# Retention scores in a hybrid decoder trunk: one plain float32 product, or three float32r products of high and low parts

## The chip, the cores and the metric

The kernel runs on one core of a Trainium2 chip. The metric is the device time of one execution in microseconds (us), the median of several runs. A core has five engines that work side by side, each with a queue of its own: TensorE (PE; its weight loads are listed as PEld), VectorE (DVE), ScalarE (ACT), GpSimd (POOL) and SyncE (SP). Matrix products land in PSUM, a small memory of eight banks, out of which ACT and DVE read them.

## What is computed

Two layers of a decoder trunk over 512 tokens of width 1024, all in float32. Each layer is a mixer and then a gated MLP with a short convolution. The mixer projects the tokens once (2560 columns) and feeds three groups of heads from it: differential attention, retention, and a causal pooling mixer. The change is in retention, which goes through the sequence in four chunks of 128 tokens with four heads of 32 query and key columns:

```python
def step(state, inp):
    qi, ki, vi = inp
    inner = jnp.einsum('bhqd,bhkd->bhqk', qi, ki) * decay
    o = (jnp.einsum('bhqk,bhkv->bhqv', inner, vi)
         + jnp.einsum('bhqd,bhdv->bhqv', qi * xi, state))
    state = state * chunk_decay + jnp.einsum('bhkd,bhkv->bhdv', ki * zeta, vi)
    return state, o
```

`inner` before the decay is what is called the scores here.

## The kernel before

Most of the work is weight products. A weight tile of 128x1024 is loaded by SP, ACT rounds it to float32r (the high part, L298 or L287), and DVE subtracts that from the original (the low part, L299 or L288). A product in nearly full precision is then three float32r products: high with high, high with low, low with high (`mm3`, L467). The projections of the mixer, its output projection and the two of the MLP run one after the other in this form. `emit_split` keeps six such tiles ahead.

The attention, retention and pooling work is cut into small steps, written as generators, that are put between the weight products. The order of TensorE is written out by hand: `in_order` (L328) ties each product to the one before it. When a step is put in is decided while the program is built: a counter `now` goes up by one for each 512 columns of weight products (`serve`, L362), and each step has a due time in the table `PLACE` (L45). When its due time is reached and the steps that it needs have been issued, it goes into the queues. On ACT, DVE and POOL the tile framework orders the queues by priority, in which these steps are ahead of the weight work by 300, and it places the semaphores by the buffers that instructions share.

Retention of chunk c consists of four such steps, for which `PLACE` has due times r1 (395, 431, 465, 513 for chunks 0 to 3), r2 (425, 439, 479, 523), r3 (427, 445, 497, 531) and r4 (491, 500, 545, 553):
- `ret_1` (L761): two transposes on TensorE put the chunk's queries and keys, turned, side by side into one PSUM bank `b`. POOL clears `qe`, a block matrix of 128x512; ACT copies the four heads of the queries onto its diagonal blocks (L773, 32 partitions each). DVE copies the keys (L774), multiplies the queries by xi (L775) and the untransposed keys by zeta (L770).
- `ret_2` (L778): one product of 128x512 in plain float32 gives the scores of all four heads; DVE multiplies them by the decay (L782), over `qe`.
- `ret_3` (L784): products with the values and the state, the new state, and the norm of the output.
- `ret_4` (L812): the output is transposed, gated, and split into high and low parts (L823, L824).

Steps of others stand between them: attention's `unit_a` to `unit_e` (scores, transposes, values), the gate `gu_done` (L669), and `pool_f`. `k_split` (L635) cuts attention's keys: for each half of the partitions ACT rounds the high part out of a PSUM bank (L637), and DVE subtracts it from the same bank (L638). `finish_token` (L449) squares a bank on ACT (L454) and multiplies it by the gain on DVE (L456).

Buffers: `t4` (L183) gives tiles of 128x1024 out of a pool of two; `ret_1` takes one for qe, the keys, and the two scaled copies. `t2` (L177) gives tiles of 128x512 from eight slots that are taken in turn by role; role p1 has two slots, used by attention's probabilities and by squares and temporaries of `unit_c`, `ret_3` and `ret_4`. PSUM banks of role b are two, in turn.

Of the kernel before, what the change touches and what calls it, by code (L numbers as in the profile page):

```python
# [11 lines left out]
F32 = mybir.dt.float32  # L12
F32R = mybir.dt.float32r
I32 = mybir.dt.int32
AF = mybir.ActivationFunctionType
ALU = mybir.AluOpType
# [4 lines left out]
P = 128  # L21
D = 1024
# [115 lines left out]
def tile_trunk(ctx: ExitStack, tc: tile.TileContext, x, xt, win, wout, wup, wdown, gpost, par, lam, const, out):  # L138
    nc = tc.nc
    te, ve, se, ge, sy = nc.tensor, nc.vector, nc.scalar, nc.gpsimd, nc.sync  # L140
# [4 lines left out]
    t4p = ctx.enter_context(tc.tile_pool(name="t4p", bufs=2))  # L145
    t2p = ctx.enter_context(tc.tile_pool(name="t2p", bufs=1))
# [6 lines left out]
    def nm(s):  # L153
        uid[0] += 1
        return f"{s}_{uid[0]}"
# [6 lines left out]
    def bank(role, shape=(P, 512)):  # L162
        k = role
        if role in BANKS:
            k = BANKS[role][took[role] % len(BANKS[role])]
            took[role] += 1
        return pp.tile(list(shape), F32, tag=f"bank{k}", name=nm(f"ps_{role}"), bufs=1)
# [6 lines left out]
    ROLES = {"any": list(range(8)), "p0": [0, 1, 2], "p1": [3, 4], "aT": [5, 6], "on": [7], "g": [2]}  # L174
    turn = {r: 0 for r in ROLES}

    def t2(role="any", w=512):  # L177
        ring = ROLES[role]
        k = ring[turn[role] % len(ring)]
        turn[role] += 1  # L180
        return t2p.tile([P, w], F32, tag=f"t2_{k}", name=nm("t2"), padded_shape=[P, 512])

    def t4():  # L183
        return t4p.tile([P, D], F32, tag="t4", name=nm("t4"))

    def small(w):
        return sp.tile([P, w], F32, tag="sm", name=nm("sm"), padded_shape=[P, 16])
# [7 lines left out]
    def C(name):  # L195
        lo, hi = _CONST_AT[name]
        return cst[:, lo:hi]
# [130 lines left out]
    def in_order(r):  # L328
        if last_pe[0] is not None:
            tc.add_manual_dep(r.ins, last_pe[0].ins.name, ORDER, reason="order of TensorE")  # L330
        last_pe[0] = r

    def mm(out, lhsT, rhs, **k):
        in_order(te.matmul(out, lhsT=lhsT, rhs=rhs, **k))  # L334

    def tr(out, in_):
        in_order(te.transpose(out, in_, ident))  # L337
# [71 lines left out]
    def head_rsqrt(ss, n, width):  # L409
        v = small(n)  # L410
        ve.tensor_scalar(v, ss, 1.0 / width, EPS, op0=ALU.mult, op1=ALU.add)
        return rsqrt(v, n)


    def norm_token(t):
        ss = small(2)
        h = t4()
        cut = [slice(0, 512), slice(512, D)]
        for i, c in enumerate(cut):
            se.activation(h[:, c], xs[:, t, c], AF.Square, scale=SQ, accum_out=ss[:, i:i + 1])  # L420
        r = row_rsqrt(ss)
        se.activation(h[:, cut[0]], xs[:, t, cut[0]], AF.Copy, scale=r)
        ve.tensor_scalar(h[:, cut[1]], xs[:, t, cut[1]], r, None, op0=ALU.mult)
        return h
# [4 lines left out]
    def row_factors(t):  # L429
        ss = small(2)  # L430
        for i in range(2):
            scr = t2()
            se.activation(scr, xs[:, t, i * 512:(i + 1) * 512], AF.Square, scale=SQ, accum_out=ss[:, i:i + 1])
        row[t] = tiny.tile([P, 1], F32, tag=f"row{t}", name=nm("row"))
        row_rsqrt(ss, row[t])
# [13 lines left out]
    def finish_token(t, ys, gp):  # L449
        ss = small(2)  # L450
        yg = [t2(), t2()]
        for h in range(2):
            scr = t2()
            se.activation(scr, ys[h], AF.Square, scale=SQ, accum_out=ss[:, h:h + 1])  # L454
        for h in range(2):
            ve.tensor_tensor(out=yg[h], in0=ys[h], in1=gp[:, h * 512:(h + 1) * 512], op=ALU.mult)  # L456
        r = row_rsqrt(ss)
        for h in range(2):
            xh = xs[:, t, h * 512:(h + 1) * 512]
            ve.scalar_tensor_tensor(xh, yg[h], r, xh, op0=ALU.mult, op1=ALU.add)  # L460
# [47 lines left out]
    def load_xt(j):  # L508
        xparts[j] = t4()
        sy.dma_start(xparts[j], xt[j])  # L510
# [8 lines left out]

    raws[0] = rp.tile([P, D], F32, tag="raw", name=nm("raw"))  # L520
    xparts[0] = t4()
    state["dma"] = 1
    load_params(0, se)
# [37 lines left out]
    for l in range(DEPTH):  # L561
# [195 lines left out]
        ret = {}  # L757
        st_bd = [None]
        on_of = {}

        def ret_1(c):  # L761
            tok = rtok[c // 2][:, c % 2, :]
            b = bank("b")
            tr(b[:, 0:P], tok[:, 0:P])
            tr(b[:, P:2 * P], tok[:, P:2 * P])
            w = t4()
            qe, kq, kz = w[:, 0:512], w[:, 512:768], w[:, 768:896]
            ge.memset(qe, 0.0)
            zeta = C("zeta").unsqueeze(2).to_broadcast([P, 4, 32])
            ve.tensor_tensor(out=kz.rearrange("p (h d) -> p h d", h=4), in0=tok[:, 128:256].rearrange("p (h d) -> p h d", h=4), in1=zeta, op=ALU.mult)  # L770
            for h in range(4):
                sl = slice(32 * h, 32 * h + 32)
                se.copy(qe[sl, h * P:(h + 1) * P], b[sl, 0:P])  # L773
            ve.tensor_copy(kq[:, 0:P], b[:, P:2 * P])  # L774
            ve.tensor_tensor(out=kq[:, P:2 * P], in0=b[:, 0:P], in1=C("xi"), op=ALU.mult)  # L775
            ret[c] = (qe, kq, kz)

        def ret_2(c):  # L778
            qe, kq, kz = ret[c]
            b = bank("b")  # L780
            mm(b, lhsT=kq[:, 0:P], rhs=qe, start=True, stop=True)
            ve.tensor_tensor(out=qe, in0=b, in1=C("decay"), op=ALU.mult)  # L782

        def ret_3(c):  # L784
            ind, kq, kz = ret.pop(c)
            b = bank("b")
            if c > 0:
                mm(b[:, 0:256], lhsT=kq[:, P:2 * P], rhs=st_bd[0], start=True, stop=False, skip_group_check=True)
            for h in range(4):
                mm(b[:, 64 * h:64 * h + 64], lhsT=ind[:, h * P:(h + 1) * P], rhs=vr[:, c, 64 * h:64 * h + 64],  # L790
                          start=(c == 0), stop=True, skip_group_check=True)
            if c < NT - 1:
                bu = bank("b")
                mm(bu[:, 0:256], lhsT=kz, rhs=vr[:, c, :], start=True, stop=True)
                ns = one.tile([P, 256], F32, tag="state", name=nm("state"), bufs=2)
                bm = C("bm").unsqueeze(2).to_broadcast([P, 4, 64])
                ve.tensor_tensor(out=ns.rearrange("p (h d) -> p h d", h=4), in0=bu[:, 0:256].rearrange("p (h d) -> p h d", h=4), in1=bm, op=ALU.mult)
                if c > 0:
                    ve.scalar_tensor_tensor(ns, st_bd[0], C("cd"), ns, op0=ALU.mult, op1=ALU.add)
                st_bd[0] = ns  # L800
            oc = rtok[c // 2][:, c % 2, :]
            ov = oc.rearrange("p (h d) -> p h d", h=4)
            se.copy(oc, b[:, 0:256])
            sq = t2("p1", 256)
            se.activation(sq, oc, AF.Square)
            ss = small(4)
            ve.tensor_reduce(ss, sq.rearrange("p (h d) -> p h d", h=4), axis=AX.X, op=ALU.add)
            r = head_rsqrt(ss, 4, 64)
            ve.tensor_tensor(out=ov, in0=ov, in1=r.unsqueeze(2).to_broadcast([P, 4, 64]), op=ALU.mult)
            on_of[c] = oc  # L810
# [74 lines left out]
        def retention(c):  # L885
            yield (l, "r1", c), ((l, "r", c), *[(l, "r3", c - 2)] * (c >= 2), *[(l, "r1", c - 1)] * (c >= 1))
            ret_1(c)
            done.add((l, "r1", c))
            yield (l, "r2", c), ()
            ret_2(c)  # L890
            yield (l, "r3", c), [(l, "r3", c - 1)] * (c >= 1)
            ret_3(c)
            done.add((l, "r3", c))
            yield (l, "r4", c), ((l, "g", 0), (l, "g", 1), (l, "a", 4 * c + 3))
            ret_4(c)
            done.add((l, "r4", c))
# [256 lines left out]
```

## Time and profile before

| | us |
|---|---|
| median of three runs | 1147.39 |
| lowest and highest run | 1146.5, 1148.37 |
| the profiled execution | 1147.81 |
| its span, first to last instruction | 1146.0 |

The granted TensorE clock was 0.998 of full speed over the span. How to read the profile's lines: a group gives line, engine, operation, output and inputs by their names, shape and number, then busy time and mean duration of one; a timeline gives start and duration in us, with the idle time before in brackets and what ended it. `t` stands for any tile of t2 or t4, `ps_b` for a bank of role b, `ps_m` for one of the projections. The line of a source view has the shortest, median and longest duration in ns. In a windows view stand, after the stretch and its length, the busy times of PE, PEld, DVE, ACT and POOL with the number of instructions, then the granted clock, the DMA share and GB/s. Matmuls are pipelined: their starts overlap, and differences are taken between ends.

### The profile page before, as it was taken

Reading aid. Unit: us, or ns where it says so; the run is one execution under the profiler, and the core shown is the slowest. Engines: PE = TensorE matmul, PEld = TensorE weight load, DVE = VectorE, ACT = ScalarE, POOL = GpSimd, SP = SyncE. Lnnn points to the kernel's source line nnn. Section 1 sums busy time; section 2 is a strip of 40 time slices with the busy share of each in tenths; the row PEclk is TensorE's granted clock in tenths of the full one; section 3 lists DMA queues with packets and bytes.
Section 4 is the critical chain, followed back from the end, with each engine's and each line's share of the span. In section 5 each row is a group of like instructions: output and inputs, shape, how many; then the busy total and the mean of one; then the engine's idle time right before and its main releaser. Section 6 shows DMA issues by size and latency. Waiting matters only on the chain.

```text
span 1146.0 us, 14829 instructions
## 1 busy us (share of the span) xinstructions
PE 1134.1 (99%) x5474; PEld 944.3 (82%) x5474; DVE 739.4 (65%) x1669; ACT 546.9 (48%) x1049; POOL 12.0 (1%) x20
## 2 busy tenths in 40 slices
PE   9999999999999999999999999999999999999997
PEld 6788878988888888888888888789888888888885
DVE  6988796776566457423777896876856645663224
ACT  6965544564454345313466754454645434442211
POOL 1000000000000000000000000000000000000000
PEclk9999999999999999999999999999999999999999
DMA  8411131332322222224023111313332223222311
GB/s 326 146 58 56 55 118 36 111 129 97 106 92 93 102 101 100 93 97 142 6 101 116 59 63 46 110 45 121 113 108 93 91 97 107 93 88 98 107 38 56
DMA packets 31320, 109.22 MB, mean 95 GB/s; under 512 B 3728, under 2 KB 4240, under 8 KB 31248
## 3 DMA queue, kind: packets, MB, share of 16 engines
q1 hardware_dynamic: 29808, 105.11, 26.7%
q10 hardware_dynamic: 1440, 3.17, 0.8%
q8 instruction: 43, 0.70, 0.2%
q14 instruction: 29, 0.24, 0.1%
HBM read 106.16 MB, written 2.10 MB: 94 GB/s over the span
## 4 chain that ended last, share of the span: by engine, by line
PE 89%; DVE 4%; ACT 4%; DMA 2%; issue 1%; SPq 0%; DVEq 0%; ACTq 0%
PE ps L334 72%; PE ps_m L334 10%; PE ps_b L334 2%; PE ps_o L334 2%; PE ps_b L337 2%; PE ps_s L334 1%; PE ps L337 1%; DMA rt<-in_lam 1%; DMA raw<-in_wout 1%; DVE ks L638 1%; ACT wa L298 1%; DMA raw<-in_win 1%; ACT t L610 0%; ACT t L701 0%; ACT c L628 0%
## 5 line engine op out<-in xcount | busy, mean ns | idle before, releaser
L334 PE MATMUL ps<-ht,wb 128*128 128x512 f32 (+1 forms) x1176 | 305.0, 368 | 0.0
L334 PE MATMUL ps<-ht,wa 128*128 128x512 f32 (+1 forms) x1176 | 304.8, 367 | 0.0
L334 PEld LDWEIGHTS ps<-ht,wa 128*128 128x128 f32 x1176 | 210.3, 188 | 36.5
L334 PEld LDWEIGHTS ps<-ht,wb 128*128 128x128 f32 x1176 | 210.1, 188 | 36.5
L299 DVE SCALAR_TENSOR_TENSOR wa<-raw,par,wa 128x512 fp32r<-128x512 f32 x128 | 95.7, 748 | 144.6 <-ACT wa L298 144.4
L298 ACT ACTIVATE wa<-raw,par 128x512 fp32r<-128x512 f32 x128 | 92.2, 721 | 185.1 <-PE ps L334 173.4
L334 PE MATMUL ps<-wa,c 128*128 128x512 f32 x448 | 126.3, 394 | 0.0
L334 PE MATMUL ps<-wa,ht 128*128 128x512 f32 x352 | 98.2, 392 | 1.3 <-ACT ht L516 1.1
L288 DVE TENSOR_TENSOR wb<-raw,wa 128x1024 fp32r<-128x1024 f32 x38 | 46.6, 1225 | 81.9 <-ACT wa L287 81.9
L299 DVE SCALAR_TENSOR_TENSOR wb<-raw,par,wb 128x512 fp32r<-128x512 f32 x128 | 95.7, 747 | 4.9 <-ACT wb L298 4.8
L334 PEld LDWEIGHTS ps<-wa,c 128*128 128x128 f32 x448 | 83.6, 188 | 18.0 <-issue 1.0
L298 ACT ACTIVATE wb<-raw,par 128x512 fp32r<-128x512 f32 x128 | 91.9, 720 | 4.3 <-PE ps L334 3.1
L334 PE MATMUL ps_m<-wa,ht 128*128 128x512 f32 x288 | 83.6, 398 | 0.0
L334 PE MATMUL ps_m<-wb,ht 128*128 128x512 f32 x288 | 83.3, 397 | 0.0
L287 ACT CAST wa<-raw 128x1024 fp32r<-128x1024 f32 x38 | 40.0, 1052 | 86.7 <-PE ps L334 86.7
L1023 ACT ACTIVATE t<-ps,par 128x512 f32<-128x512 f32 x88 | 67.5, 774 | 24.9 <-PE ps L334 24.9
L334 PEld LDWEIGHTS ps<-wa,ht 128*128 128x128 f32 x352 | 65.7, 188 | 16.1 <-ACT ht L516 1.9
L1024 DVE SCALAR_TENSOR_TENSOR t<-ps,par,t 128x511 f32<-128x511 f32 x88 | 65.2, 745 | 11.8 <-ACT t L1023 11.7
L334 PE MATMUL ps<-wb,c 128*128 128x512 f32 x224 | 71.8, 397 | 0.0
L334 PE MATMUL ps<-wb,ht 128*128 128x512 f32 x224 | 66.3, 389 | 0.0
L1025 DVE SCALAR_TENSOR_TENSOR t<-ps,par,t 128x510 f32<-128x510 f32 x88 | 65.1, 745 | 1.3
L334 PEld LDWEIGHTS ps_m<-wb,ht 128*128 128x128 f32 x288 | 52.5, 188 | 10.1
(185 smaller groups left out, 1415.8 us busy)
## 6 DMA issues: line engine op xcount, KB each, us to landing
raw<-in_wup SPq DMA_DIRECT2D x88, 512.0 KB, 3.5
raw<-in_wdown SPq DMA_DIRECT2D x44, 512.0 KB, 3.4
raw<-in_win SPq DMA_DIRECT2D x39, 512.0 KB, 3.5
raw<-in_wout SPq DMA_DIRECT2D x16, 512.0 KB, 3.5
xs<-in_x SPq DMA_DIRECT2D x4, 512.0 KB, 9.6
gain<-in_gpost ACTq DMA_DIRECT2D x4, 512.0 KB, 4.5
t<-in_xt SPq DMA_DIRECT2D x3, 512.0 KB, 5.8
out<-xs SPq DMA_DIRECT2D x4, 256.0 KB, 2.0
```

Of the source, the lines that this page charges most:

```text
L287: se.copy(h, r)
L288: ve.tensor_tensor(out=lo, in0=r, in1=h.bitcast(F32), op=ALU.subtract)
L298: se.activation(a, x, AF.Copy, scale=sc)
L299: ve.scalar_tensor_tensor(b, x, sc, a.bitcast(F32), op0=ALU.mult, op1=ALU.subtract)
L334: in_order(te.matmul(out, lhsT=lhsT, rhs=rhs, **k))
L337: in_order(te.transpose(out, in_, ident))
L638: ve.tensor_tensor(out=ks[o, :, m, sl], in0=bv[r], in1=ks[r, :, m, sl].bitcast(F32), op=ALU.subtract)
L1023: se.activation(acc, ps, AF.Identity, bias=conv[:, f, 3:4], scale=conv[:, f, 2:3])
L1024: ve.scalar_tensor_tensor(acc[:, 1:S], ps[:, 0:S - 1], conv[:, f, 1:2], acc[:, 1:S], op0=ALU.mult, op1=ALU.add)
L1025: ve.scalar_tensor_tensor(acc[:, 2:S], ps[:, 0:S - 2], conv[:, f, 0:1], acc[:, 2:S], op0=ALU.mult, op1=ALU.add)
```

## The change

The scores are made as the weight products are: queries and keys are cut into a high part in float32r and the remainder, and three float32r products are added up in the bank. `ret_1` takes a second t4 tile, in float32r, of which the left half `qe` holds the queries' high parts and the right half `ql2` their low parts, both cleared by POOL; and a p1 tile `kk` with the keys' high part `kh` and low part `kl`. The decayed scores go to `ind`, in the first tile, and no longer over `qe`. In each head ACT rounds the high part out of bank b and DVE subtracts it from the same place of the bank; then the same for the keys. The keys' copy moves from DVE to ACT. `ret_3` differs only in names, and the due times are as before.

```diff
-    def t2(role="any", w=512):
+    def t2(role="any", w=512, dtype=F32):
         ...
-        return t2p.tile([P, w], F32, tag=f"t2_{k}", name=nm("t2"), padded_shape=[P, 512])
+        return t2p.tile([P, w], dtype, tag=f"t2_{k}", name=nm("t2"), padded_shape=[P, 512])
-    def t4():
-        return t4p.tile([P, D], F32, tag="t4", name=nm("t4"))
+    def t4(dtype=F32):
+        return t4p.tile([P, D], dtype, tag="t4", name=nm("t4"))
...
             tr(b[:, 0:P], tok[:, 0:P])
             tr(b[:, P:2 * P], tok[:, P:2 * P])
-            w = t4()
-            qe, kq, kz = w[:, 0:512], w[:, 512:768], w[:, 768:896]
-            ge.memset(qe, 0.0)
+            w, qe, kk = t4(), t4(F32R), t2("p1", 256, F32R)
+            ind, qx, kz = w[:, 0:512], w[:, 512:640], w[:, 640:768]
+            qe, ql2 = qe[:, 0:512], qe[:, 512:D]
+            kh, kl = kk[:, 0:P], kk[:, P:2 * P]
+            for x in (qe, ql2):
+                ge.memset(x.bitcast(F32), 0.0)
...
             for h in range(4):
                 sl = slice(32 * h, 32 * h + 32)
-                se.copy(qe[sl, h * P:(h + 1) * P], b[sl, 0:P])
-            ve.tensor_copy(kq[:, 0:P], b[:, P:2 * P])
-            ve.tensor_tensor(out=kq[:, P:2 * P], in0=b[:, 0:P], in1=C("xi"), op=ALU.mult)
-            ret[c] = (qe, kq, kz)
+                cut = slice(h * P, (h + 1) * P)
+                se.copy(qe[sl, cut], b[sl, 0:P])
+                ve.tensor_tensor(out=ql2[sl, cut], in0=b[sl, 0:P], in1=qe[sl, cut].bitcast(F32), op=ALU.subtract)
+            se.copy(kh, b[:, P:2 * P])
+            ve.tensor_tensor(out=kl, in0=b[:, P:2 * P], in1=kh.bitcast(F32), op=ALU.subtract)
+            ve.tensor_tensor(out=qx, in0=b[:, 0:P], in1=C("xi"), op=ALU.mult)
+            ret[c] = (qe, ql2, kh, kl, ind, qx, kz)

         def ret_2(c):
-            qe, kq, kz = ret[c]
+            qe, ql2, kh, kl, ind, qx, kz = ret.pop(c)
             b = bank("b")
-            mm(b, lhsT=kq[:, 0:P], rhs=qe, start=True, stop=True)
-            ve.tensor_tensor(out=qe, in0=b, in1=C("decay"), op=ALU.mult)
+            for n, (x, y) in enumerate(((kh, qe), (kh, ql2), (kl, qe))):
+                mm(b, lhsT=x, rhs=y, start=(n == 0), stop=(n == 2))
+            ve.tensor_tensor(out=ind, in0=b, in1=C("decay"), op=ALU.mult)
+            ret[c] = (ind, qx, kz)
```

More of the change, by code (lines that the diff above doesn't have):

```diff
@@ L772, in ret_1 @@
                 sl = slice(32 * h, 32 * h + 32)
-                se.copy(qe[sl, h * P:(h + 1) * P], b[sl, 0:P])
-            ve.tensor_copy(kq[:, 0:P], b[:, P:2 * P])
-            ve.tensor_tensor(out=kq[:, P:2 * P], in0=b[:, 0:P], in1=C("xi"), op=ALU.mult)
-            ret[c] = (qe, kq, kz)
+                cut = slice(h * P, (h + 1) * P)
[5 more added lines that the diff above has]
+            ret[c] = (qe, ql2, kh, kl, ind, qx, kz)
         def ret_2(c):
-            qe, kq, kz = ret[c]
+            qe, ql2, kh, kl, ind, qx, kz = ret.pop(c)
             b = bank("b")
-            mm(b, lhsT=kq[:, 0:P], rhs=qe, start=True, stop=True)
-            ve.tensor_tensor(out=qe, in0=b, in1=C("decay"), op=ALU.mult)
+            for n, (x, y) in enumerate(((kh, qe), (kh, ql2), (kl, qe))):
+                mm(b, lhsT=x, rhs=y, start=(n == 0), stop=(n == 2))
+            ve.tensor_tensor(out=ind, in0=b, in1=C("decay"), op=ALU.mult)
+            ret[c] = (ind, qx, kz)
         def ret_3(c):
-            ind, kq, kz = ret.pop(c)
+            ind, qx, kz = ret.pop(c)
             b = bank("b")
             if c > 0:
-                mm(b[:, 0:256], lhsT=kq[:, P:2 * P], rhs=st_bd[0], start=True, stop=False, skip_group_check=True)
+                mm(b[:, 0:256], lhsT=qx, rhs=st_bd[0], start=True, stop=False, skip_group_check=True)
             for h in range(4):
```

## The prediction

> **What bounds the kernel now.** I read the page's first part, then its chain, then the queues around the eight score products.
>
> ```profile
> span 1146.0 us, 14829 instructions
> ...
> PE 1134.1 (99%) x5474; PEld 944.3 (82%) x5474; DVE 739.4 (65%) x1669; ACT 546.9 (48%) x1049; POOL 12.0 (1%) x20
> ...
> PE 89%; DVE 4%; ACT 4%; DMA 2%; issue 1%; SPq 0%; DVEq 0%; ACTq 0%
> ```
>
> TensorE is busy in 99% of the span and carries 89% of the chain. Its order is written out by hand and stays as it is. So two things count: TensorE time that is removed, and any time for which TensorE must now wait, because nothing later has slack to take a wait back. DVE's 65% is a mean. In the six stretches of 6 us in which chunks 1, 2 and 3 make their scores (three for each layer) the windows view shows DVE in the third figure after the comma:
>
> ```profile
> 140.00:146.00 6.00, 6.00 (x30) 4.63 (x29) 5.78 (x27) 3.33 (x8) 0.53 (x1) 1.00 0.00 0
> 151.00:157.00 6.00, 6.00 (x27) 4.61 (x26) 5.97 (x16) 3.29 (x7) 0.00 (x0) 1.00 0.64 203
> 166.00:172.00 6.00, 6.00 (x27) 4.39 (x26) 5.93 (x22) 1.34 (x5) 0.00 (x0) 1.00 0.31 100
> 706.50:712.50 6.00, 6.00 (x30) 4.63 (x28) 5.69 (x27) 3.41 (x8) 0.53 (x1) 1.00 0.00 1
> 717.50:723.50 6.00, 6.00 (x27) 4.57 (x26) 6.00 (x16) 3.39 (x7) 0.00 (x0) 1.00 0.66 199
> 732.50:738.50 6.00, 6.00 (x26) 4.41 (x25) 5.89 (x21) 1.34 (x5) 0.00 (x0) 1.00 0.28 93
> ```
>
> DVE is full there, 5.69 to 6.00 of 6, and both layers look alike. I work on layer 0 and double. The granted clock is 1.00 throughout, so it plays no part.
>
> **Part 1: the products on TensorE.** The timeline of chunk 0's score (start, duration, then the group):
>
> ```profile
> 134.57 0.93 PE L334 MATMUL ps_m<-ht,wa 128*128 128x512 f32 x3
> 135.34 0.86 PE L334 MATMUL ps_m<-ht,wb 128*128 128x512 f32 x3
> 136.04 1.02 PE L334 MATMUL ps_b<-t 128*128 128x512 f32 x2
> 136.50 0.80 PE L334 MATMUL ps_m<-ht,wa 128*128 128x512 f32 x1
> ```
>
> One plain product is two instructions. Ends are the measure, since starts overlap: the group before ends at 136.20 and the score at 137.06, so it takes 0.86 us. Three float32r products of the same 128x512 size end 0.70 apart (135.50 to 136.20). Saved: 0.16 us for a score, 1.3 us for eight. No other TensorE work changes.
>
> **Part 2: cutting into high and low parts.** Before, ret_1 made four ACT copies, then two DVE operations. Now each ACT copy of a head is followed by a DVE subtraction which reads the same PSUM bank, then come kh on ACT, kl and qx on DVE. What do two engines do that read one bank?
>
> ```profile
> L456 DVE TENSOR_TENSOR t<-ps,gain x32: 677/686/693, 184.7 to 1138.9; 128x512 f32<-128x512 f32 x32
> ...
>   ACT t L454: 43.7, 11
> ...
> 59.79 0.69 DVE L638 TENSOR_TENSOR ks<-ps_b,ks 64x512 fp32r<-64x512 f32 x1
> ...
> 60.51 0.58 ACT L637 CAST ks<-ps_b 64x512 fp32r<-64x512 f32 x1 [0.87 <-DVE ks L638]
> ```
>
> The second line is from the list of what ended the idle time before L456. L456 multiplies a bank by the gain; ACT's L454 squares the same bank into another tile. Neither uses the other's result, yet DVE idled 43.7 us, 11 times, until ACT was done. The other direction: in k_split, ACT's L637 of the upper partitions began at 60.51, 0.03 us after DVE's L638 of the lower ones ended (59.79 + 0.69 = 60.48). So reads of one bank by ACT and DVE take turns. Then the new chain can't overlap: copy 0, subtraction 0, copy 1, and so on to copy 3, subtraction 3, kh. The prices of its links:
>
> ```profile
> L773 ACT COPY t<-ps_b x32: 236/257/261, 126.7 to 734.6; 32x128 f32<-32x128 f32 x32
> ...
> L774 DVE COPY t<-ps_b x8: 279/285/292, 128.1 to 735.1; 128x128 f32<-128x128 f32 x8
> ```
>
> A copy is 0.257 us. The 32x128 subtraction isn't in this trace; the nearest is L774, also 128 columns out of PSUM, 0.285. Below it is nothing that small on DVE with PSUM input; if it took only the copy's 0.257, six links would give back 0.1 us a chunk. With 0.03 for each hand-over a round is 0.257 + 0.03 + 0.285 + 0.03 = 0.60 us. From the start T of subtraction 0 to the end of kh: 0.285 + 0.03 + three rounds (1.81) + 0.257 = 2.38 us.
>
> Now the three tight chunks. First chunk 1, in the timeline:
>
> ```profile
> 140.09 0.53 POOL L768 MEMSET t<- 128x512 f32 x1 [75.50 <-ACT rtok L803]
> ...
> 140.50 0.38 PE L337 MATMUL ps_b<-cst,rtok 128*128 128x128 f32 x2
> ...
> 140.98 1.06 ACT L773 COPY t<-ps_b 32x128 f32<-32x128 f32 x4 [0.43 <-PE ps_b L337]
> ...
> 141.71 0.15 DVE L397 TENSOR_TENSOR sm<-sm,sm 128x4 f32<-128x4 f32 x1
> ...
> 142.07 0.29 DVE L774 COPY t<-ps_b 128x128 f32<-128x128 f32 x1 [0.21 <-ACT t L773]
> ...
> 142.80 1.02 PE L334 MATMUL ps_b<-t 128*128 128x512 f32 x2
> ```
>
> The transposes L337 end at 140.88 and the score starts at 142.80, in line with the products before it: 1.9 us for the whole cut. Then chunks 2 and 3:
>
> ```profile
> 152.66 1.04 ACT L773 COPY t<-ps_b 32x128 f32<-32x128 f32 x4
> ...
> 152.82 1.28 DVE L299 SCALAR_TENSOR_TENSOR wb<-raw,ws,wa 128x1024 fp32r<-128x1024 f32 x1
> ...
> 154.09 0.29 DVE L774 COPY t<-ps_b 128x128 f32<-128x128 f32 x1
> 154.29 0.15 DVE L397 TENSOR_TENSOR sm<-sm,sm 128x4 f32<-128x4 f32 x1
> ...
> 155.04 0.59 PE L334 MATMUL ps_b<-t 128*128 128x512 f32 x1
> ...
> 167.20 1.06 ACT L773 COPY t<-ps_b 32x128 f32<-32x128 f32 x4
> ...
> 168.10 0.42 DVE L824 TENSOR_TENSOR c<-t,c 128x256 fp32r<-128x256 f32 x1
> ...
> 168.51 0.28 DVE L774 COPY t<-ps_b 128x128 f32<-128x128 f32 x1
> ...
> 168.94 1.10 PE L334 MATMUL ps_b<-t 128*128 128x512 f32 x2
> ```
>
> Chunk 3's score already waits a little: it lasts 1.10 instead of 1.02, so it really begins at 170.04 - 1.02 = 169.02, which is 0.23 after its operand's copy (L774) ended at 168.79. That 0.23 is my price from last operand to score.
>
> T is where DVE's other work lets subtraction 0 in. I choose for it a place that DVE's queue has today after the first copy has ended (its start plus 0.257): in chunk 1 141.71, where L397 stands; in chunk 2 154.09, where L774 stands behind a weight split (L299) of 1.28 us; in chunk 3 168.51, where L774 stands behind the retention output's low part (L824). New start of the score = T + 2.38 + 0.23:
> - chunk 1: 144.32 instead of 142.80, a wait of 1.5 us;
> - chunk 2: 156.70 instead of 155.04, 1.7 us;
> - chunk 3: 171.12 instead of 169.02, 2.1 us;
> - chunk 0: T = 128.1 (first L774), ready at 130.7, score at 136.04: 5 us spare, no wait.
>
> Sum 5.3 us a layer, 10.6 us for two. Minus 1.3 saved: **+9.3 us**. kl is ready 0.03 + 0.285 after kh, and the two products before it cover 0.47, so it adds nothing unless other DVE work slips in before it.
>
> Bounds. If DVE takes each subtraction at once, T is 0.29 behind the copies' start (141.27, 152.95, 167.49) and the waits are 1.1, 0.5 and 1.1: 2.7 a layer, net +4.1. If on top of my sum one other piece of 512 columns gets between two links in each chunk (0.69, as L638 above), it is 2.1 more a layer, net +13.5. Below nothing the whole cannot go by more than Part 1's 1.3, since nothing else is removed from TensorE and the cut only adds work to ACT, DVE and POOL. My value is nearer the middle because T is taken from rows.
>
> **Part 3: the rest.** The second memset on POOL (0.53) is in front of subtraction 0, not of the copies: chunk 1's pair would run 140.09 to 141.15, before 141.71; POOL is 1% busy and nothing else is queued there. If it were late, at most 0.5 us a chunk. ret_1 now takes both t4 buffers, so chunk c+1 needs chunk c's qe and w free; both are released by r3(c) at the latest, which stands ahead of r1(c+1) in the order for every c, and the memset at 140.09 is already one that follows r3(0). Cost nothing, with the same 0.5 as bound. kk in the p1 ring: between r1 and r2 of a chunk at most one other p1 tile is asked for, nothing waits. Behind the waiting instructions stand, on ACT, the gate's tanh (L677) and weight splits (L298); on DVE, the gate's multiplication (L678), the low halves of splits (L299), and then the decay multiplication (L782), for which r3's products wait. All these are later by as much as TensorE is, so I count no second wait. DVE's added work, some 1.1 us a chunk (four subtractions at 0.285), falls into the waits.
>
> The profiled execution took 1147.81 us around its span of 1146.0, 0.42 above the median of the runs, 1147.39. 1147.81 + 9.3 = 1157.1; against the median 1156.7, which is my time.
>
> **Rivals.**
> 1. *Turns are taken by part of a bank.* If the four copies may run on while subtractions read other partitions, only kh, which reads all, waits for subtraction 3. Then the subtractions follow at 0.20, the step from L774 to the next operation in chunk 2 (154.09 to 154.29). Subtraction 3 can begin at 142.07, 154.69 and 169.11, and kh and the score come 0.285 + 0.03 + 0.257 + 0.23 = 0.80 later: chunk 1 at 142.87, chunk 2 at 155.49, chunk 3 at 169.91; waits 0.1, 0.45 and 0.9, 1.4 a layer, net +1.5: 1148.9, no change that shows. It decides if copy 1 starts before subtraction 0 ends. Against it: L637 at 60.51 and L638 touch different halves of the partitions and still took turns; but both write one tile, so that row isn't clean. The Trainium skill (PSUM — Partial Sum Buffer, section on bank collisions) says just this: two engines need to be kept apart only within the same bank and group of 32 partitions, and each head here is such a group. By that rule this rival would hold; the row at 60.51 speaks the other way. 15%.
> 2. *The cut is covered* because the queues are reordered so that the score's operands come first. Only Part 1 is left: 1147.4 - 1.3 = 1146.1. Chunk 1's 1.9 us against 2.6 speaks against it. 7%.
> 3. *Other work gets into the links more often*: weight splits such as the 1.28 us one in chunk 2 fill the idle time between links and run over. Two pieces of 0.69 a chunk are 4.1 a layer: +17.6, 1165.0. It decides from the second piece that gets in. For it: DVE is full. Against: each piece taken early is one less later. 13%.
>
> The forecast itself has 65%.
>
> **The numbers.** About 0.2% (2.3 us) is what a measurement of this kernel can tell from no change. The range goes from 1148.5, just below rival 1, past the bounds +4.1 (1151.5) and +13.5 (1160.9) to 1163.0, midway from the latter to rival 3. Of the chances it leaves out rival 2 (7%), half of rival 3 (6.5%) and a third of rival 1 (5%). Faster by over 0.2%: only as the tail of rival 2, 3%. Within: the rest of rival 2 and most of rival 1, 16%. Slower: 81%.
>
> **What would show it.** Right: in ret_1, ACT copies and DVE subtractions alternate with idle time on ACT ended by DVE; the first score product of chunks 1 to 3 has a wait of 1.5 to 2.1 us ended by ACT (kh); eight times three products at 0.23 each; TensorE's busy time 1.3 us less of work. Wrong: four copies in a row as now with no DVE wait between (rival 1), or scores in line with their neighbours (rival 2).

## The result and the profile after

| | before | after |
|---|---|---|
| median, us | 1147.34 (6 runs) | 1176.85 (6 runs) |
| lowest and highest | 1146.5, 1148.37 | 1175.15, 1178.71 |
| the profiled execution, us | 1147.81 | 1178.71 |
| its span, us | 1146.0 | 1176.9 |
| granted TensorE clock over the span | 0.998 | 0.986 |

The change costs 29.5 us: the ratio is 1.0254, with an interval of 1.0243 to 1.0265. That is on the side that was forecast, but 20.2 us above the time that was forecast and 13.9 above the top of the range.

The page of after, its span, busy times, and the clock in 40 slices (tenths):

```profile
span 1176.9 us, 14897 instructions
...
PE 1143.2 (97%) x5482; PEld 952.7 (81%) x5482; DVE 751.9 (64%) x1701; ACT 549.9 (47%) x1057; POOL 15.7 (1%) x28
...
PEclk9999979999999999999999999899999999999999
```

Two things are new. TensorE was busy 99% of the span and is busy 97%. And its busy time rose by 9.1 us, from 1134.1 to 1143.2, although the change takes work from it. The clock row says why: a 7 in slice 6 (147 to 177 us) and an 8 in slice 26 (736 to 765 us), which are the stretches of retention in the two layers.

Not all of the difference between these two profiled executions is the change's. The first transposes of chunk 0 end at 128.93 us instead of 126.63, so 2.3 us were there before any changed step ran. Early on TensorE waited 1.67 us here and 1.11 before, and from 21.08 to 24.49 us the clock was 0.50, which the profile of before doesn't have. The profiled execution is the slowest of the six, 1.9 us above their median.

The list of TensorE's waits shows where the 2% went. After the line number stands who ended the wait, then the total in us, the number of times, and the longest:

```profile
PEld ps_b L334 <- issue: 23.6, 6, 6.5
...
PE ps_b L334 <- issue: 12.1, 2, 6.1
PE ps_b L334 <- ACT t L780: 9.1, 4, 3.8
```

Six waits are the six tight scores, chunks 1 to 3 of both layers. L780 is the copy of kh. The matmuls stood still for 12.1 + 9.1 = 21.2 us ahead of them, their weight loads for 23.6 (4.4, 6.5 and 0.9 us a layer; some expectations below name these). The list of before has no wait of a score that it puts down to the cut.

The timelines of TensorE at the scores of chunks 1, 2 and 3 in layer 0 (start, duration, group, idle time before):

```profile
148.91 1.62 PE L334 MATMUL ps_b<-t,t 128*128 128x512 f32 x3 [3.85 <-ACT t L780]
```

```profile
169.67 1.62 PE L334 MATMUL ps_b<-t,t 128*128 128x512 f32 x3 [6.02 <-issue]
```

```profile
186.18 0.93 PE L334 MATMUL ps_b<-t,t 128*128 128x512 f32 x3 [0.69 <-ACT t L780]
```

The waits are 3.85, 6.02 and 0.69 us, where 1.5, 1.7 and 2.1 were forecast. And the same three products last 1.62 us in chunks 1 and 2, 0.93 in chunk 3. The windows of after around chunks 1 and 2, the last one from layer 1, give the clock in the figure after POOL's:

```profile
145.10:149.10 4.00, 0.19 (x1) 0.22 (x2) 3.71 (x20) 1.93 (x4) 0.00 (x0) 0.78 0.00 0
149.50:153.50 4.00, 4.00 (x11) 3.14 (x10) 1.98 (x2) 0.00 (x0) 0.98 (x2) 0.50 0.01 4
163.50:170.00 6.50, 0.48 (x2) 0.36 (x2) 5.46 (x16) 4.80 (x9) 0.00 (x0) 0.83 0.45 141
170.00:174.00 4.00, 4.00 (x10) 3.11 (x10) 3.94 (x9) 0.62 (x1) 0.98 (x2) 0.50 0.17 49
...
751.00:755.00 4.00, 4.00 (x11) 3.12 (x10) 3.94 (x7) 0.63 (x1) 0.98 (x2) 0.51 0.24 73
```

While TensorE waits (first and third row) it does next to nothing; in the 4 us behind each wait it is busy throughout, at half clock. This is the other part of the loss, and no step of the prediction had it.

Now the chain of the cut. ACT in chunk 1 of after; L778 is a copy of a head, L779 a subtraction, L780 kh:

```profile
143.11 0.26 ACT L778 CAST t<-ps_b 32x128 fp32r<-32x128 f32 x1 [0.40 <-PE ps_b L337]
143.56 0.63 ACT L677 ACTIVATE sg<-t 128x512 f32<-128x512 f32 x1 [0.19 <-DVE t L676]
144.22 0.26 ACT L778 CAST t<-ps_b 32x128 fp32r<-32x128 f32 x1
145.10 1.15 ACT L298 ACTIVATE wa<-raw,ws 128x1024 fp32r<-128x1024 f32 x1 [0.63 <-PE ps_m L334]
146.28 0.26 ACT L778 CAST t<-ps_b 32x128 fp32r<-32x128 f32 x1
147.59 0.26 ACT L778 CAST t<-ps_b 32x128 fp32r<-32x128 f32 x1 [1.05 <-DVE t L779]
148.50 0.27 ACT L780 CAST t<-ps_b 128x128 fp32r<-128x128 f32 x1 [0.66 <-DVE t L779]
```

and DVE in the same chunk:

```profile
143.91 0.27 DVE L779 TENSOR_TENSOR t<-ps_b,t 32x128 fp32r<-32x128 f32 x1
...
144.25 0.67 DVE L678 SCALAR_TENSOR_TENSOR sg<-sg,t 128x512 f32<-128x512 f32 x1
...
145.11 0.28 DVE L779 TENSOR_TENSOR t<-ps_b,t 32x128 fp32r<-32x128 f32 x1
...
146.47 0.69 DVE L738 TENSOR_TENSOR t<-ps_o,sm 128x512 f32<-128x512 f32 x1
...
147.27 0.29 DVE L779 TENSOR_TENSOR t<-ps_b,t 32x128 fp32r<-32x128 f32 x1
```

Read the two together. Copy 0, subtraction 0, copy 1, subtraction 1: one engine holds the bank, the other waits, as forecast. But into the gap on ACT between copy 0 and copy 1 went the gate's tanh (L677), between copies 1 and 2 a weight split (L298, 1.15 us); into the gaps on DVE went the gate's multiplication (L678), attention's L738 and eighteen operations of some 0.15 us. Each is in front of the next link in its engine's queue, and where it isn't done in time, the link comes late. From copy 0 to the end of kh it is 148.77 - 143.11 = 5.66 us, where the forecast has 3.1 (140.98 to 144.09).

Which pieces cost something is seen by setting each link's start against the end of the link before it; undisturbed it follows 0.03 us later. The tanh cost nothing: copy 1 starts 0.04 us after subtraction 0 ended (143.91 + 0.27 = 144.18). The split cost copy 2 0.9 us. The rest, 2.1 us, is DVE's: its four subtractions come 0.5, 0.6, 0.7 and 0.3 us late. Chunk 2 is worse, and there it is the other engine; ACT:

```profile
161.10 0.24 ACT L778 CAST t<-ps_b 32x128 fp32r<-32x128 f32 x1
163.01 1.15 ACT L298 ACTIVATE space<-raw,ws 128x1024 fp32r<-128x1024 f32 x1 [1.67 <-DMA raw<-in_wout]
164.18 0.26 ACT L778 CAST t<-ps_b 32x128 fp32r<-32x128 f32 x1
165.57 1.15 ACT L298 ACTIVATE space<-raw,ws 128x1024 fp32r<-128x1024 f32 x1 [1.13 <-DMA raw<-in_wout]
166.74 0.26 ACT L778 CAST t<-ps_b 32x128 fp32r<-32x128 f32 x1
...
169.31 0.27 ACT L780 CAST t<-ps_b 128x128 fp32r<-128x128 f32 x1
```

8.48 us instead of 3.8. Between the first and last copy stand four weight splits and a copy of the pooling part on ACT, a split (L299, 1.28), two of pooling's L681 and four of its L842 (0.67 to 0.69 each) on DVE. By the same reckoning ACT's pieces cost 4.2 us and DVE's 1.6. And two of ACT's splits had to wait for the transfer of their own weights, 1.67 and 1.13 us, with the next copy behind them in the queue: the cut waited for weights that it has nothing to do with. Layer 1 shows the same two (1.59 and 1.29 us). In chunk 3 little else is left to get in:

```profile
183.26 0.26 ACT L778 CAST t<-ps_b 32x128 fp32r<-32x128 f32 x1 [2.15 <-PE ps_b L337]
183.93 0.26 ACT L778 CAST t<-ps_b 32x128 fp32r<-32x128 f32 x1 [0.42 <-DVE t L779]
...
185.15 0.26 ACT L778 CAST t<-ps_b 32x128 fp32r<-32x128 f32 x1 [0.35 <-DVE t L779]
185.77 0.27 ACT L780 CAST t<-ps_b 128x128 fp32r<-128x128 f32 x1 [0.36 <-DVE t L779]
```

Here the rounds are 0.61 us, the forecast's 0.60, and the chain lasts 2.78; from the start of subtraction 0 (183.62) to the end of kh it is 2.42.

### The profile page after: what moved, and what is told of

It reads as the page before. It is cut to its first block, busy times and chain, and to the rows that moved or that the text cites. A ratio compares the mean times of both kernels' runs of the same rounds, so it can differ in the third digit from the quotient of the medians.

```text
span 1176.9 us, 14897 instructions
## 1 busy us (share of the span) xinstructions
PE 1143.2 (97%) x5482; PEld 952.7 (81%) x5482; DVE 751.9 (64%) x1701; ACT 549.9 (47%) x1057; POOL 15.7 (1%) x28
## 4 chain that ended last, share of the span: by engine, by line
PE 91%; DVE 4%; ACT 2%; issue 2%; DMA 1%; SPq 0%; DVEq 0%; ACTq 0%
PE ps L334 71%; PE ps_m L334 12%; PE ps_b L334 2%; PE ps_b L337 2%; PE ps_o L334 1%; PE ps_s L334 1%; DMA raw<-in_win 1%; PE ps L337 1%; DVE ks L638 1%; DVE t L779 0%; ACT t L701 0%; DVE sm L699 0%; DVE ps_s L698 0%; ACT wa L298 0%; ACT ks L637 0%
## 5 line engine op out<-in xcount | busy, mean ns | idle before, releaser
L299 DVE SCALAR_TENSOR_TENSOR wa<-raw,par,wa 128x512 fp32r<-128x512 f32 x128 | 95.7, 748 | 146.1 <-ACT wa L298 145.8
L298 ACT ACTIVATE wa<-raw,par 128x512 fp32r<-128x512 f32 x128 | 92.2, 721 | 186.3 <-PE ps L334 173.4
L299 DVE SCALAR_TENSOR_TENSOR wb<-raw,par,wb 128x512 fp32r<-128x512 f32 x128 | 95.7, 748 | 5.0 <-ACT wb L298 4.9
L298 ACT ACTIVATE wb<-raw,par 128x512 fp32r<-128x512 f32 x128 | 91.8, 719 | 4.3 <-PE ps L334 3.2
```

Of the source, the lines that this page charges most:

```text
L298: se.activation(a, x, AF.Copy, scale=sc)
L299: ve.scalar_tensor_tensor(b, x, sc, a.bitcast(F32), op0=ALU.mult, op1=ALU.subtract)
```

## The experiments

Theory A, after the result: ACT and DVE take turns on the one bank, every turn lets other queued work in front of the next link, TensorE waits for the end of the chain, and behind a wait of some 4 us it runs at half clock. Rivals: the added operations cost by their mere number; or the buffers and clears (second t4 tile, `kk`, second memset) do; or the chain is slow because of DVE's load, turns or no turns. Times are medians; the kernel before beside them had 1147.2 to 1147.6.

**The copies first.** The loop is split, so that ACT makes all five copies before DVE's first subtraction; the operations are the same.

```diff
                 se.copy(qe[sl, cut], b[sl, 0:P])
-                ve.tensor_tensor(out=ql2[sl, cut], in0=b[sl, 0:P], in1=qe[sl, cut].bitcast(F32), op=ALU.subtract)
             se.copy(kh, b[:, P:2 * P])
+            for h in range(4):
+                (the same subtraction)
```

> The same instructions as the changed kernel, but ret_1 makes all five ACT copies first and the five DVE subtractions after them. Theory (ACT and DVE take turns on one PSUM bank, and other work gets between the links of that chain): one hand-over is left, the waits at the scores of chunks 1 to 3 fall from 4.4, 6.5 and 0.9 us to at most 0.5 to 1 each, the clock stays at 1.0, time 1147 to 1151 us. Rival (DVE is full, and the five subtractions are too much work for it, in whatever order): the work is the same, so the time stays above 1170.

Measured 1152.49 us (1151.74 to 1152.68), 1.0042 of before, interval 1.0029 to 1.0054: 24.4 us of the 29.5 are gone, and the time is 1.5 above the range that was expected. ACT in chunk 1:

```profile
140.73 1.06 ACT L778 CAST t<-ps_b 32x128 fp32r<-32x128 f32 x4 [0.39 <-PE ps_b L337]
141.81 0.27 ACT L779 CAST t<-ps_b 128x128 fp32r<-128x128 f32 x1
```

The copies run on as before the change, in 1.35 us, and the granted clock is 0.998 again. So the number of operations isn't the cause; their order on the bank is. Most of what is left is in one row of TensorE's waits (here L783 is the subtraction):

```profile
PE ps_b L334 <- DVE t L783: 4.8, 6, 1.3
```

The second product needs the queries' low parts, and the four subtractions now stand one behind the other in DVE's full queue.

**Two banks.** The same two transposes are made a second time into a bank of another role, and DVE reads that one; ACT and DVE share no bank. The order of the statements is that of the change.

```diff
+            b2 = bank("s" if c < 2 else "o")
+            tr(b2[:, 0:P], tok[:, 0:P])
+            tr(b2[:, P:2 * P], tok[:, P:2 * P])
-                ve.tensor_tensor(out=ql2[sl, cut], in0=b[sl, 0:P], ...
+                ve.tensor_tensor(out=ql2[sl, cut], in0=b2[sl, 0:P], ...
```

> The changed kernel with its order of instructions in ret_1 as it is, but queries and keys are transposed a second time into another PSUM bank (of role s for chunks 0 and 1, o for 2 and 3), out of which DVE reads, while ACT reads the first. Adds 16 transposes of 0.11 us. Theory (the shared bank makes the turns): ACT's copies run on without a wait for DVE, no wait of over 1 us at the scores, time 1147.3 - 1.3 + 1.8 plus 0 to 1 us a chunk = 1148 to 1154 us. Rival (each subtraction must follow its copy anyway, or DVE's load): waits stay, above 1170.

Measured 1156.51 us (1155.76 to 1158.24), 1.0081, interval 1.0067 to 1.0095. The copies ran on in 1.37 to 1.39 us although the subtractions stand between them in the program, and the scores waited for 1.6 us in all in four times. The time still misses its range. The largest wait left is of the experiment's own making: the second transposes of chunk 0 came while the borrowed bank was still in use, on the timeline of TensorE:

```profile
128.97 0.44 PE L337 MATMUL ps_s<-cst,rtok 128*128 128x128 f32 x2 [2.20 <-ACT t L701]
```

Twice that is 4.4 us; without it the time would be near 1152 (an estimate: 1156.5 - 4.4).

**Turns and nothing else.** The kernel before, plain product and all, with one thing added: behind each ACT copy of a head DVE copies one column of that head out of the bank into a scratch tile. No cutting, no new product, no new buffer but that scratch tile.

```diff
                 se.copy(qe[sl, h * P:(h + 1) * P], b[sl, 0:P])
+                ve.tensor_copy(small(1)[sl, 0:1], b[sl, 0:1])
```

> The kernel before, plain product and all, with one more DVE instruction behind each of the four ACT copies of the queries: a copy of a single column of the same PSUM bank into a scratch tile. It adds 4 x 8 instructions of well under 0.2 us to DVE and nothing else. Theory (taking turns on the bank is enough): the copies wait for DVE and DVE's other work gets in between, the scores of chunks 1 to 3 wait 1 to 6 us each, time 1155 to 1175 us. Rival (it is the work of the subtractions, the second memset or the float32r products): within 1 us of 1147.4.

Measured 1171.96 us (1170.73 to 1172.28), 1.0208, interval 1.0194 to 1.0222: 24.8 us for 32 operations of 0.15 us, 4.9 us of work on an engine that is not the bound. ACT in chunk 1 (L773 is the copy of a head, L774 the new one-column copy):

```profile
140.72 0.25 ACT L773 COPY t<-ps_b 32x128 f32<-32x128 f32 x1 [0.44 <-PE ps_b L337]
141.17 0.63 ACT L677 ACTIVATE sg<-t 128x512 f32<-128x512 f32 x1 [0.20 <-DVE t L676]
142.02 0.26 ACT L773 COPY t<-ps_b 32x128 f32<-32x128 f32 x1 [0.22 <-DVE sm L774]
142.74 1.15 ACT L298 ACTIVATE wa<-raw,ws 128x1024 fp32r<-128x1024 f32 x1 [0.46 <-PE ps_m L334]
143.91 0.26 ACT L773 COPY t<-ps_b 32x128 f32<-32x128 f32 x1
144.94 0.26 ACT L773 COPY t<-ps_b 32x128 f32<-32x128 f32 x1 [0.78 <-DVE sm L774]
```

It is the picture of after: the same tanh and the same weight split between the same copies. The copies and the one-column reads share no result; only the bank ties them. Scores waited for 16.8 us, and the clock fell behind the waits here too (0.992 over the span). With this the buffers are out as the main cause, as the number of operations was by the copies first.

**No subtractions.** The change without its five subtractions. It leaves the low parts out and adds high times high a second time, so its scores are others than those of the change; it only shows what the rest costs.

```diff
-                ve.tensor_tensor(out=ql2[sl, cut], in0=b[sl, 0:P], ...
-            ve.tensor_tensor(out=kl, in0=b[:, P:2 * P], ...
-            for n, (x, y) in enumerate(((kh, qe), (kh, ql2), (kl, qe))):
+            for n, (x, y) in enumerate(((kh, qe), (kh, ql2), (kh, qe))):
```

> The changed kernel without the five subtractions of each chunk: the low parts are left out (the scores are high by high, high by zeros, and high by high again), all else stays: two t4 tiles, the p1 tile, two memsets on POOL, the keys' copy on ACT, three float32r products. Theory: only the saving on TensorE is left, 1147.3 - 1.3 = 1146 us, give or take 1. Rival (the two t4 tiles, the second memset or the keys' copy on ACT hold up the scores): the time stays well above 1150, with the waits at the scores ended by POOL or ACT.

Measured 1145.33 us (1144.02 to 1146.66, 11 runs), 0.9982, interval 0.9973 to 0.9991: 2.06 us under before. TensorE's list of waits has no row for a score. So second memset, second t4 tile, `kk`, kh on ACT and the three products together cost nothing and save 2.06; all of the loss hangs on the subtractions. It also marks what this form could bring here if the subtractions cost nothing.

**TensorE kept busy.** The change, with plain products of two constants, 5 in chunk 1 and 7 in chunk 2, put in front of the score into a bank that nobody reads then. They fill the wait; the chain is untouched.

```diff
             b = bank("b")
+            if c in (1, 2):
+                fill = bank("s" if c < 2 else "o")
+                for _ in range((5, 7)[c - 1]):
+                    mm(fill, lhsT=ident, rhs=C("decay"), start=True, stop=True)
```

> The changed kernel with 5 (chunk 1) and 7 (chunk 2) plain float32 products of constants into an unused bank, put on TensorE just ahead of the scores, 4.3 and 6.0 us of work in the time in which it would wait. Theory (after a wait of over 4 us TensorE runs at a granted clock of 0.5 for 3.4 to 6.8 us, which costs about 8 us of the added 29.5): the clock stays at 1.0 there and the time falls to 1168 us, give or take 2; the copies and subtractions alternate as before. Rival (the low clock costs nothing, because the queues on ACT and DVE set the pace there): 1176 us or more.

Measured 1168.73 us (1168.66 to 1169.4), 1.0187, interval 1.0173 to 1.0201: 8.1 us less than the change, for more work on TensorE. Its timeline in chunk 1, and a window right behind:

```profile
142.20 4.45 PE L334 MATMUL ps_s<-cst 128*128 128x512 f32 x10
146.21 1.13 PE L334 MATMUL ps_b<-t,t 128*128 128x512 f32 x3
```

```profile
146.00:150.00 4.00, 4.00 (x22) 3.27 (x21) 2.68 (x5) 0.07 (x1) 0.99 (x2) 1.00 0.01 4
```

The cut's chain is as long as it was (5.67 us in chunk 1), but the clock stays at 1.00 behind it, and 22 matmuls fit into 4 us where 11 did. So some 8.1 us of the 29.5 are the clock's.

**Other work held behind the cut.** In the change, all ACT and DVE work issued after a chunk's cut is ordered behind its last operation, so that it can't get between the links.

```diff
-            se.copy(kh, b[:, P:2 * P])
+            last_act = se.copy(kh, b[:, P:2 * P])
-            ve.tensor_tensor(out=qx, ...
+            last_dve = ve.tensor_tensor(out=qx, ...
+            (every later ACT instruction behind last_act, every later DVE one behind last_dve)
```

> The changed kernel with its chain of copies and subtractions as it is, but all ACT and DVE work that the program issues after a chunk's cut is tied behind the cut's last copy (ACT) and last operation (DVE). In chunks 1 and 2 the weight splits, the tanh and the pooling sums can then no longer get between the links. Theory (turns on the bank open the gaps, and other work that fills them is what makes the wait long): the chains of chunks 1 and 2 shrink from 5.7 and 8.5 us to about 3 to 4, the waits at their scores from 4.4 and 6.5 to 1 to 2 us, the clock stays at 1.0, time 1153 to 1160 us. Rival (the turns alone, ten hand-overs a chunk, cost it, whatever stands between): still 1170 to 1177.

Measured 1167.5 us (1166.58 to 1169.25), 1.0173, interval 1.0159 to 1.0187: missed. In chunk 1 the chain shrank to 4.10 us and the wait to 2.28. Chunk 2 is as it was said, with a chain of 3.01 us and no wait over 0.2 at its score. But splits that had been issued earlier were now late and got into chunk 3's chain, which grew to 8.45 us. TensorE at chunk 3's score:

```profile
175.74 1.62 PE L355 MATMUL ps_b<-t,t 128*128 128x512 f32 x3 [6.38 <-ACT t held:10]
```

**A chain with nothing in it.** As the last one, and the links of chunks 1 to 3 are also ordered behind the ACT and DVE work issued before them.

> The changed kernel with its turns on the bank as they are, but in chunks 1 to 3 the cut's links follow each other on ACT and DVE with nothing in between: work issued earlier is tied ahead of the first link, work issued later behind the last. This mends the run before in which only later work was held back and the wait moved to chunk 3. Theory (two parts: turns give 0.61 us a round, 2.8 us from the first copy to kh; what gets in between made 5.4 and 8.5 us of it in chunks 1 and 2): all chains 2.7 to 2.9 us, no low clock, waits of 1 to 3 us a chunk, since the first link now stands behind all earlier work, time 1152 to 1162 us. Rival (the turns alone make the long waits): chains as before, 1167 or more.

Measured 1182.78 us (1181.81 to 1184.84), 1.0307, interval 1.0293 to 1.0321: the slowest of all, and the expectation wrong; by its time the rival would hold. ACT in chunk 1 (all lines are the helper's; the first two rows and the last are copies 0 and 1 and kh):

```profile
140.43 0.26 ACT held:11 CAST t<-ps_b 32x128 fp32r<-32x128 f32 x1 [0.39 <-PE ps_b L365]
144.10 0.26 ACT held:11 CAST t<-ps_b 32x128 fp32r<-32x128 f32 x1 [3.41 <-DVE t held:11]
...
145.94 0.27 ACT held:11 CAST t<-ps_b 128x128 fp32r<-128x128 f32 x1 [0.36 <-DVE t held:11]
```

From the start of subtraction 0 (143.79) to the end of kh (146.21) it is 2.42 us: the forecast's 2.38 for an undisturbed chain holds, so the rival doesn't. But subtraction 0 had to wait 3.1 us behind copy 0 for DVE's backlog. The work that is kept out from between the links is then in front of them. Most of the loss is in chunk 3, where the score waits 9.04 us: copy 0 stands behind three weight splits on ACT, and ACT was idle for 4.65 and 1.33 us before two of them, until their weights had come. So this run shows how long the chain is by itself, but doesn't price the turns: it adds an order that the change hasn't got.

**Later scores.** The copies-first form with r2 at 425, 448, 483, 530 and r3 at 427, 454, 497, 538.

> The changed kernel with all copies first, as in the run that gave 1152.5, and later due times: r2 at 425, 448, 483, 530 and r3 at 427, 454, 497, 538, that is 2.1, 0.9 and 1.6 us later for the scores of chunks 1 to 3, whose first products still waited 1.6, 0.5 and 1.1 us. Theory (what is left over the run without subtractions, 1145.3, are these waits, and TensorE has weight products to do meanwhile): 1145 to 1148 us. Rival (the later steps only push the wait to r3, whose products wait for the decay, or to the retention output that the output projection needs): 1150 us or more.

Measured 1154.81 us (1154.62 to 1156.66), 1.0064, interval 1.0051 to 1.0076: missed. The waits for the subtractions went, and others took their place: 3.4 us at transposes behind L738, 1.8 and 1.6 us at products behind retention's own later steps.

**One copy and one subtraction.** ACT rounds the whole 128x256 once, DVE subtracts once, and the blocks are filled from those two tiles: the queries' high parts by ACT, the low parts by POOL. The bank changes hands once. r2 at 425, 443, 481, 525; r3 at 427, 449, 497, 533.

```diff
+            se.copy(hi, b[:, 0:2 * P])
+            ve.tensor_tensor(out=lo, in0=b[:, 0:2 * P], in1=hi.bitcast(F32), op=ALU.subtract)
-                se.copy(qe[sl, cut], b[sl, 0:P])
+                se.copy(qe[sl, cut], hi[sl, 0:P].bitcast(F32))
-                ve.tensor_tensor(out=ql2[sl, cut], in0=b[sl, 0:P], ...
+                ge.tensor_copy(ql2[sl, cut], lo[sl, 0:P].bitcast(F32))
```

> The changed kernel with one cut for queries and keys together: ACT copies the bank's 128x256 once, rounded, DVE subtracts it once, and the blocks of qe and ql2 are copied out of SBUF, the high parts by ACT and the low parts by POOL. The bank changes hands once, and DVE has two operations a chunk as before the change. r2 and r3 of chunks 1 to 3 are due 0.9, 0.5 and 0.5 us later. Theory: nothing waits for over 0.5 us, 1145 to 1148 us. Rival (POOL's block copies, or ACT's ninth to thirteenth, become the late operand): waits at the scores ended by POOL or ACT, 1149 to 1156 us.

Measured 1152.95 us (1152.35 to 1153.92), 1.0046, interval 1.0032 to 1.006: missed. The turns are gone, but now POOL's copies end the wait, 3.8 us in four times; the four of chunk 3 took

```profile
168.35 3.31 POOL L782 CAST t<-t 32x128 fp32r<-32x128 f32 x4 [9.95 <-DVE sm L398]
```

**The same with ACT for both.** `se.copy` instead of `ge.tensor_copy`.

> As the kernel that cuts queries and keys once as 128x256 (1152.95), but the low parts' blocks too are copied by ACT and not by POOL, whose copies of 128 columns took 0.28 us alone and 0.77 to 1.32 beside DVE's weight splits. Theory (POOL's slowed copies were the late operand in chunk 3, 2.0 us): waits in chunk 3 fall under 1 us, time 1147 to 1151 us. Rival (ACT, with nine copies a chunk, is later than POOL was): 1152 us or more.

Measured 1148.27 us (1147.77 to 1149.08, 11 runs), 1.0005, interval 0.9996 to 1.0014: no difference from before, and within the expected range. In chunk 1 ACT rounds in 0.38 us and fills the two sets of blocks in 1.22 and 1.20 (the second set is L785). It is the best form of the three products with all their parts that was run. What remains is 1.8 us of waits for L785.

**The same, later still.** r2 at 425, 447, 481, 528; r3 at 427, 453, 497, 536.

> As the run with one cut and all blocks copied by ACT (1148.27), whose scores still waited 0.9 us in chunk 1 and 0.45 in chunk 3, with r2 and r3 due another 0.9 us later in chunk 1 and 0.7 in chunk 3. Theory (these waits are all that is left over the run without subtractions, 1145.3): 1145.5 to 1147 us, the only form that could be shown to be faster than the plain product. Rival (DVE is full, and later scores only make the decay and the products of r3 late, as in the run with copies first and later steps): 1148 us or more.

Measured 1149.55 us (1148.49 to 1151.11, 11 runs), 1.002, interval 1.0011 to 1.0029: missed; the rival held, waits only changed places.

**Chunk 0 alone.** The change's form in chunk 0, the plain product in chunks 1 to 3.

> The changed form in chunk 0 alone, the plain product in chunks 1 to 3. Theory (chunk 0 has some 9 us between its transposes and its score, so turns and other work in them are covered): no wait at its score, within 0.2% of 1147.3, that is 1146.5 to 1148 us. Rival (what the chain delays on ACT and DVE comes back later as another wait): 1149 us or more.

Measured 1147.38 us (1146.4 to 1149.41, 11 runs), 0.9997, interval 0.9988 to 1.0005. Where 9.4 us of other products lie between transposes and score (126.29 to 135.70), the cut is free, turns and all, though other work got into this chain too: it lasts 5.7 us.

## Why the prediction was wrong

**The bound** was read rightly: TensorE had no slack, and each wait showed in the time.

**Part 1** had the right sign: no subtractions, 2.06 us saved instead of 1.3. Beyond the products, two small waits of before are gone there; one is that at chunk 3's score, which the prediction had read, the other one of 0.21 us in chunk 2, behind L820.

**Turns on the bank** were right, and are shown: the one-column reads alone bring 24.8 us, copies first or two banks take most of the loss away. A round is 0.61 us for the 0.60 forecast, the undisturbed chain 2.42 for 2.38. T was near in chunk 1: subtraction 0 starts 0.80 us behind copy 0, where the prediction has 0.73.

**Rival 1 fell.** Copy 1 (partitions 32 to 63) always came after subtraction 0 (partitions 0 to 31) had ended; in chunk 3 the idle time of 0.42 before it is put down to L779. The Trainium skill (PSUM — Partial Sum Buffer, section on bank collisions) lets two engines use one bank in different groups of 32 partitions. The traces show that this program doesn't do so, in the waits that the framework placed; whether the chip would let the links overlap if these waits went by 32 partitions was not tried. Its step of 0.20 for the subtractions was off too: with the copies first, in chunk 0, four of them took 1.19 us, some 0.30 each.

**The step that failed: what gets in between the links.** The forecast put one delay (T) in front of subtraction 0 and then let the chain run. It read DVE as full, 5.69 to 6.00 of 6, but took that as a delay once, not at each of eight hand-overs. And of ACT's tanh and splits, of DVE's gate and low halves, its Part 3 says that they stand behind the waiting instructions and are only later; in the change they ran between the links. On ACT these are splits of 1.15 us each, two of them in chunk 2 after a wait for their weights. Its upper bound allowed one piece of 0.69 in a chunk, rival 3 two; the links came 3.0 us late in all in chunk 1, 5.8 in chunk 2. Chunk 1's chain is 5.66 instead of 3.1, chunk 2's 8.48 instead of 3.8, so the waits are 3.85 and 6.02 instead of 1.5 and 1.7. Rival 3 named the mechanism; its argument against ("each piece taken early is one less later") didn't help, for TensorE waits now, whatever is saved later. In chunk 3 it is true: DVE had caught up while TensorE stood still, and the wait is 0.69, not 2.1. The sum of waits is 21.2 us where 10.6 were forecast.

**The term that was missing: the clock.** "It plays no part" was read from a trace in which TensorE never waited as long. In the retention stretches of all runs, waits of 3.67 us and more (3.85 and 6.02 here, 3.68 and 4.19 in the one-column kernel, 6.38 in the held one, 3.95 and 9.04 in the clean chain) all came with half clock; waits up to 2.28 us did not, and none lies between. The price by the filled kernel is 8.1 us. The traces give somewhat more: the same 5482 products kept TensorE busy for 1132.0 us without the subtractions and for 1143.2 after, 11.2 more. Some 1.7 of it are the early low stretch (an estimate: half of the 3.36 us of work in it), which leaves 9.5 us. The Trainium skill (TensorE: Matmul & The Clock Gate, section Part 1: The HAM clock gate) says that the clock is halved after an idle window of about 3.4 us and comes back after a busy one of that length. The runs agree with the length, 3.41 us or a multiple, but not with "idle": the traces decide, and in them a stretch that is busy in part is enough (the last section has the rows). No wait as short as the forecast ones, at most 2.1 us, lowered the clock in retention, so the first error called in the second.

**The account.** By the profiled executions the span grew by 30.9 us, of which 2.3 stand ahead of retention. The other 28.6 are 21.2 of waits and 9.5 of clock, less 2.1 saved on products and small waits. With the filled kernel's 8.1 for the clock it is 27.2 of the 29.5 between the medians; the rest isn't assigned.

**Part 3** was right in its costs: memset, buffers and `kk` cost nothing. "No second wait" held in the change: TensorE's list has no wait behind the decay multiplication. That the queues drained while TensorE stood is the likely reason, not shown. In later scores and in the kernel with one copy, second waits appeared (1.6 and 1.7 us behind the decay multiplication).

**What stays open.** That the 7.2 us between copies first (1152.49) and no subtractions (1145.33) come from DVE's queue is argued from the waits' row (4.8 us) and from the later scores, not shown by itself. Why the queues were ordered with splits and sums ahead of the links wasn't looked into. And no version with all three products was faster than before; the 2.06 us are there, but need the subtractions covered, and later due times, in three sets, only moved the waits.

## What to carry to other kernels

Where two engines read one PSUM bank, write all reads of the one before the first read of the other: at each hand-over a chain can lose what stands in front of the next link, and here chains of 2.8 us became 5.7 and 8.5. Before pricing a chain across engines, list for each link what its engine has queued at that time, on both engines, and what those pieces themselves wait for. And where a sum gives TensorE waits near 4 us, add the clock: here the wait's price rose by two fifths (8.1 on 21.2).

## What the hardware showed that I had not expected

- Half clock lasts much longer than the work that it hits first: behind a wait of 6.02 us it was still 0.50 in the stretch from 170.0 to 174.0 us, with TensorE busy throughout.
- The clock drops without 3.4 us of standstill. In chunk 1 of layer 0 it fell 2.3 us into the wait, after 3.41 us in which TensorE was busy for 1.11 (the first block, and half clock in its second row); early in the same execution 1.63 us of work in 3.41 (17.67 to 21.08 us) were too few as well. In the two-bank kernel (the second block) 1.92 of 3.41 kept it at 1.00. All these stretches lie on the grid of 3.41 us on which the clock changes of their execution lie. What counts in these traces is the work in such a stretch, with the limit somewhere between 1.63 and 1.92.

```profile
143.96:147.37 3.41, 1.11 (x5) 0.57 (x4) 3.28 (x21) 1.89 (x4) 0.00 (x0) 1.00 0.00 0
147.37:150.79 3.42, 1.88 (x5) 1.52 (x6) 2.10 (x9) 0.52 (x2) 0.14 (x1) 0.50 0.00 0
```

```profile
124.86:128.27 3.41, 1.92 (x11) 1.37 (x9) 3.41 (x11) 1.91 (x7) 0.00 (x0) 1.00 0.21 85
128.27:131.68 3.41, 2.71 (x18) 2.44 (x19) 1.97 (x8) 1.32 (x4) 0.00 (x0) 1.00 0.00 0
```

- 32 reads of a single column, 0.154 us each, made the kernel 2.1% slower (ratio 1.0208, interval 1.0194 to 1.0222).
- DVE operations on different groups of 32 partitions don't overlap: 1.19 us for four of 32x128, while two of 128x128 behind them (129.55 and 129.76 us) start 0.21 apart. The Trainium skill (VectorE: DVE Perf Modes, section Two Vector instructions with no wait between them) has the rule: an operation that changes the group starts when all earlier ones have finished.
- A POOL copy of 32x128 within SBUF lasts 0.28 us at best and up to 1.33 (median 0.288 of 32); the longest, in chunk 3 (0.77 to 1.33), ran beside DVE's weight splits, and one of 0.82 in chunk 1 beside the gate's multiplication (L678). That these DVE operations are the cause was not tried.
